# Modulation of a two-layer backbone step: from matmuls on TensorE to dot products on VectorE

## The chip, the core and the metric

The kernel runs on one core of a Trainium2 chip. Its engines run side by side, each in the order of its own queue: TensorE (PE in the profile; matmuls and transposes, results in PSUM), VectorE (DVE), ScalarE (ACT) and GpSimd (POOL). Loads are issued by SyncE (SP) and, for gathers, by GpSimd. The metric is the device time of one execution in microseconds (us).

## The reference

One step of a backbone of two layers on 384 tokens (128 context tokens, 256 latent tokens) of 1024 columns, all in float32. Each layer has a mixer and an expert stage, and each of both is modulated by a shift, a scale and a gate that depend on a conditioning vector: `c_ctx` for the context tokens, `c` for the latent ones.

```python
def adaln(cond, w, b):
    m = jax.nn.silu(cond) @ w + b                 # 1024 -> 6 * 1024
    return jnp.split(m[..., None, :], 6, axis=-1)

def modulate(x, shift, scale):
    return layer_norm(x) * (1 + scale) + shift
...
    # a layer, for either group of tokens
    h = modulate(x, shift1, scale1)
    p = h @ w_in                  # columns for three token mixers (A, B, C) and their gates
    ...                           # A: Mamba-2 scan, B: neighbourhood attention, C: grouped-query attention
    x = layer_norm(alpha * x + gate1 * mix, ...)
    ...                           # PEER: product-key routing, then 128 experts' rows per token
    x = layer_norm(alpha * x + gate2 * ffn, ...)
```

So the modulation itself is 6 vectors ("parts" 0 to 5: shift1, scale1, gate1, shift2, scale2, gate2) of 1024 numbers, for 2 layers and 2 conditioning vectors. Its cost is the weight `w_mod`: 2 x 1024 x 6144 floats, 50 MB.

## The kernel before

A layer is run in this order: the norm and modulation of its input (called the LN phase here), the mixer, `mix_out` with its norm, the routing of the PEER stage, and the PEER stage's loop over experts, which is bound by transfers. In the profiled run mixer 0 lies at about 50 to 490 us, the PEER loop of layer 0 at 740 to 1520, mixer 1 at 1560 to 1995, the PEER loop of layer 1 from 2240 on.

A mixer works through 52 blocks of 128 columns of `w_in`. For each block `load_w` (L205 ff) issues one load of 512 KB on SP's queue into a slot of the ring "w" (8 slots, which all weight loads share). `proj3` splits the block into a high and a low part: ScalarE's copy `uh` (L222), and the subtraction `ul` (L224) on VectorE (on GpSimd for the first N_FIRST = 3 blocks of a mixer). The ring "u" of splits has 3 slots. Then come 24 matmuls of 128 by 384 (L368 to L370). `split` serves `w_branch` too, in the loop of `branch` over the gate blocks. Between the blocks lies the work of the three mixers A, B and C, convolution and scan first. Each engine's order is written out at build time by a scheduler, so instructions of neighbouring steps are interleaved.

The modulation is made of 48 units (`adaln_unit`, L253), each for 256 columns: two loads of `w_mod`, 8 matmuls with the conditioning vectors as weights, `condT` (L259), a ScalarE copy `modp` (L261), two small matmuls that turn the result into columns (L265), and two ScalarE additions of the bias into `mcol` (L268). `mcol` is then read by the norms as per-channel columns.

The units are placed by `adaln(n, ...)`: 8 in the LN phase of layer 0 (shift1 and scale1 of the first mixer, two before every second channel block k); one after every second `w_in` block, in `blocks` (L373), up to N_FILL = (16, 8) in the two mixers; 4 behind the third `mix_out` of layer 0 (N_AD); 10 in the routing of layer 0, one in each `tick` from b = 6 on; and the last 2 at the same place as N_AD in layer 1.

Of the kernel before, what the change touches and what calls it, by code (L numbers as in the profile page):

```python
# [18 lines left out]
D = 1024  # L19
# [21 lines left out]
N_FILL = (16, 8)  # L41
N_AD = (4, 4)
N_END = 0
# [10 lines left out]
R_AD = 4  # L54
# [55 lines left out]

CAND = []
# [44 lines left out]
def hybrid_step(ctx: ExitStack, tc: tile.TileContext, A, O):  # L156
# [45 lines left out]
    mcol = mk(outer, [128, DEPTH, 6, KD, 2], "mcol")  # L202
# [25 lines left out]
    fill_ps, fill_n, first = [None], [0], [0]  # L228


    def cond_prep(sp, ps1):
        cond = mk(sp, [16, 128], "cond")
        dma(out=cond[0:8, :], in_=A["c_ctx"].rearrange("(k p) -> k p", p=128))
        dma(out=cond[8:16, :], in_=A["c"].rearrange("o (k p) -> (o k) p", p=128))
        V.memset(condT, 0.0)
        ps = mk(ps1, [128, 512], "pt")
        T.transpose(ps[:, :16], cond, ident[:16, :16])
        th = mk(sp, [128, 16], "cth")
        S.activation(th, ps[:, :16], AF.Tanh, scale=0.5)
        cc = mk(sp, [128, 16], "cc")  # L240
        S.activation(cc, ps[:, :16], AF.Copy, scale=0.5)
        V.scalar_tensor_tensor(condT[:, :, 0:2].rearrange("p k c -> p c k"), th.rearrange("p (c k) -> p c k", c=2), 1.0,
                               cc.rearrange("p (c k) -> p c k", c=2), op0=ALU.add, op1=ALU.mult)
        for l in range(DEPTH):
            bm = mk(sp, [48, 128], "bm", bufs=2)
            dma(out=bm, in_=A["b_mod"][l].rearrange("(k p) -> k p", p=128))
            ps = mk(ps1, [128, 512], "pt")
            T.transpose(ps[:, :48], bm, ident[:48, :48])
            V.tensor_copy(bmT[:, l], ps[:, :48])
            for part in (1, 4):  # L250
                V.tensor_scalar(bmT[:, l, part * KD:(part + 1) * KD], bmT[:, l, part * KD:(part + 1) * KD], 1.0, None, op0=ALU.add)

    def adaln_unit(l, part, hb, ps1, tags):  # L253

        w = load_k(A["w_mod"][l, part * 4 + hb])
        ps = mk(ps1, [128, 512], tags[0])
        for k in range(KD):
            q = k % 4
            T.matmul(ps[32 * q:32 * q + 32, :256], condT[:, k, :], w[k], start=(k < 4), stop=(k >= 4), tile_position=(0, 32 * q))  # L259
        mp = mk(outer, [128, 256], "modp", bufs=2)  # L260
# [3 lines left out]
        for a in range(2):  # L264
            T.matmul(pt[:, 2 * a:2 * a + 2], mp[:, a * 128:(a + 1) * 128], sel, start=True, stop=True)  # L265
        c = part * KD + 2 * hb
        for a in range(2):
            S.activation(mcol[:, l, part, 2 * hb + a, :], pt[:, 2 * a:2 * a + 2], AF.Identity, bias=bmT[:, l, c + a:c + a + 1])  # L268

    todo = []  # L270
    for l, ps in ((0, (0, 1)), (0, (2,)), (0, (3, 4)), (1, (0, 1)), (0, (5,)), (1, (2,)), (1, (3, 4)), (1, (5,))):
        todo += [(l, part, hb) for hb in range(4) for part in ps]
# [12 lines left out]

    def mod_rows(l, part, j, dst, ps1, tag, scale=1.0):

        for hb in range(2):
            ps = mk(ps1, [128, 512], tag)
            for a in range(4):  # L290
                T.matmul(ps[:, a * 128:(a + 1) * 128], mcol[:, l, part, hb * 4 + a, j:j + 1].to_broadcast([128, 128]), ident,
# [29 lines left out]
    def ln_mod_T(l, t, ish, isc, sp, xt, ps1, tag, raw, then=None):  # L321
# [3 lines left out]
        for hb in range(2):  # L325
# [5 lines left out]
            if hb == 0 or t < MOD_V:  # L331
                for q in range(4):
                    k = hb * 4 + q
                    S.activation(raw[:, k, :], ps[:, q * 128:(q + 1) * 128], AF.Identity, bias=mcol[:, l, ish, k, j:j + 1],
                                 scale=mcol[:, l, isc, k, j:j + 1])
            else:
                V.tensor_tensor(raw[:, ks, :], ps.rearrange("p (k t) -> p k t", k=4), mcol[:, l, isc, ks, j][:, :, None].to_broadcast([128, 4, 128]), op=ALU.mult)
# [1012 lines left out]
```

## Time and profile before

| | us |
|---|---|
| median of 3 runs | 3023.25 (3023.19 to 3025.1) |
| profiled execution | 3023.89 |
| its span | 3021.8 |
| TensorE busy | 2880.1 (95%) |
| VectorE busy | 2314.3 (77%) |
| ScalarE busy | 1398.6 (46%) |
| GpSimd busy | 820.5 (27%) |

The busy shares are means over stages with different bounds. The mean busy share of the DMA engines is under one half in the mixers and near full in the PEER loops. Matmuls are pipelined and their ends are modelled, so durations of neighbouring matmuls overlap in the rows; the distance from start to start is the pace.

### The profile page before, as it was taken

Reading aid. Unit: us, or ns where it says so; the run is one execution under the profiler, and the core shown is the slowest. Engines: PE = TensorE matmul, PEld = TensorE weight load, DVE = VectorE, ACT = ScalarE, POOL = GpSimd, SP = SyncE. Lnnn points to the kernel's source line nnn. Section 1 sums busy time; section 2 is a strip of 40 time slices with the busy share of each in tenths; the row PEclk is TensorE's granted clock in tenths of the full one; section 3 lists DMA queues with packets and bytes.
Section 4 is the critical chain, followed back from the end, with each engine's and each line's share of the span. In section 5 each row is a group of like instructions: output and inputs, shape, how many; then the busy total and the mean of one; then the engine's idle time right before and its main releaser. Section 6 shows DMA issues by size and latency. Waiting matters only on the chain. (4 is left out here: it accounts for less than half of the span.)

```text
span 3021.8 us, 48665 instructions
## 1 busy us (share of the span) xinstructions
PE 2880.1 (95%) x17953; PEld 2496.8 (83%) x17953; DVE 2314.3 (77%) x4888; ACT 1398.6 (46%) x2861; POOL 820.5 (27%) x566
## 2 busy tenths in 40 slices
PE   7999999999889999999969999999987999999996
PEld 5888889878779999998858888898876899999985
DVE  3745554599669999998977456446996999999988
ACT  4544542324864444444445445432168444444443
POOL 0000000101334445554530000000023444455554
PEclk9999999999999999999979999999999999999998
DMA  7445322464999999999934332124469999999994
GB/s 245 156 152 153 84 65 90 154 227 146 334 343 418 393 388 396 396 390 369 385 100 153 119 96 76 64 91 133 154 212 366 412 395 392 396 394 392 395 365 166
DMA packets 299328, 767.09 MB, mean 254 GB/s; under 512 B 42770, under 2 KB 113874, under 8 KB 299090
## 3 DMA queue, kind: packets, MB, share of 16 engines
q1 hardware_dynamic: 225362, 495.51, 46.0%
q0 software_dynamic: 73728, 268.47, 23.4%
q8 instruction: 141, 2.31, 0.3%
q14 instruction: 97, 0.79, 0.1%
HBM read 726.92 MB, written 36.96 MB: 253 GB/s over the span
## 5 line engine op out<-in xcount | busy, mean ns | idle before, releaser
L1052 POOL DMA_INDIRECT prow<-in_peer_u,ei x256 | 361.5, 1412 | 765.2 <-DVE prow L1057 521.6
L1063 POOL DMA_INDIRECT prow<-in_peer_v,ei x256 | 379.8, 1483 | 352.4 <-DVE tn L1068 310.8
L222 ACT CAST vh<-w 128x1024 fp32r<-128x1024 f32 x256 | 268.8, 1050 | 367.2 <-issue 285.6
L1162 PE MATMUL hp<-hh,uh 128*128 128x256 f32 x1488 | 433.8, 292 | 0.0
L1163 PE MATMUL hp<-hl,uh 128*128 128x256 f32 x1488 | 417.2, 280 | 0.0
L1164 PE MATMUL hp<-hh,ul 128*128 128x256 f32 x1488 | 416.8, 280 | 0.0
L1240 PE MATMUL out<-vh,al 128*128 128x512 f32 x1024 | 400.4, 393 | 3.6 <-DVE al L1225 3.6
L1239 PE MATMUL out<-vl,ah 128*128 128x512 f32 x1024 | 398.4, 391 | 3.1 <-DVE vl L224 3.1
L1238 PE MATMUL out<-vh,ah 128*128 128x512 f32 x1024 | 391.0, 398 | 1.4 <-ACT ah L1223 1.4
L224 DVE TENSOR_TENSOR vl<-w,vh 128x1024 fp32r<-128x1024 f32 x256 | 315.5, 1232 | 62.0 <-ACT vh L222 61.3
L1068 DVE SCALAR_TENSOR_TENSOR tn<-prow,pact,tn 128x1024 f32<-128x1024 f32 x254 | 325.0, 1280 | 2.7
L1150 ACT CAST uh<-w 128x1024 fp32r<-128x1024 f32 x186 | 195.4, 1051 | 251.7 <-PE hp L1163 243.0
L368 PE MATMUL pp<-hh,uh 128*128 128x384 f32 (+1 forms) x848 | 300.1, 354 | 8.9 <-ACT uh L222 4.7
L1057 DVE SCALAR_TENSOR_TENSOR prow<-prow,tn 128x1024 f32<-128x1024 f32 x256 | 302.2, 1218 | 0.3 <-DMA prow<-in_peer_u,ei 0.3
L370 PE MATMUL pp<-hh,ul 128*128 128x384 f32 (+1 forms) x848 | 296.3, 349 | 1.4 <-POOL ul L224 1.4
L1159 PE MATMUL hp<-hs,w 128*128 128x256 f32 x1120 | 266.5, 394 | 30.7 <-DMA w<-in_peer_uT 30.7
L369 PE MATMUL pp<-hl,uh 128*128 128x384 f32 (+1 forms) x848 | 295.0, 348 | 0.2 <-DVE xr L494 0.2
L1162 PEld LDWEIGHTS hp<-hh,uh 128*128 128x128 f32 x1488 | 281.3, 189 | 0.0
L1163 PEld LDWEIGHTS hp<-hl,uh 128*128 128x128 f32 x1488 | 281.2, 189 | 0.0
L1164 PEld LDWEIGHTS hp<-hh,ul 128*128 128x128 f32 x1488 | 280.4, 188 | 0.0
L1159 PEld LDWEIGHTS hp<-hs,w 128*128 128x128 f32 x1120 | 216.1, 197 | 63.0 <-DMA w<-in_peer_uT 33.5
L351 POOL TENSOR_TENSOR res<-res,lg 128x384 f32<-128x384 f32 x6 | 9.6, 1594 | 939.7 <-ACT res L313 939.7
(405 smaller groups left out, 5843.0 us busy)
## 6 DMA issues: line engine op xcount, KB each, us to landing
w<-in_peer_uT SPq DMA_DIRECT2D x256, 512.0 KB, 6.9
w<-in_peer_v SPq DMA_DIRECT2D x256, 512.0 KB, 7.2
w<-in_w_in SPq DMA_DIRECT2D x104, 512.0 KB, 3.7
w<-in_w_mod SPq DMA_DIRECT2D x96, 512.0 KB, 4.4
gd<-w SPq DMA_DIRECT2D x64, 512.0 KB, 6.1
gt<-gd SPq DMA_DIRECT2D x64, 512.0 KB, 7.4
w<-in_peer_wq SPq DMA_DIRECT2D x32, 512.0 KB, 4.4
w<-in_w_branch SPq DMA_DIRECT2D x24, 512.0 KB, 3.7
```

The costliest lines, as they stand in the source:

```text
L224: e.tensor_tensor(lo, src, hi.bitcast(F32), op=ALU.subtract)
L1052: G.indirect_dma_start(out=row, out_offset=None, in_=utab, in_offset=bass.IndirectOffsetOnAxis(ap=ei[:, j:j + 1], axis=0))
L1057: V.scalar_tensor_tensor(row, row, 1.0, tn, op0=ALU.mult, op1=ALU.mult, accum_out=hd[:, j:j + 1])
L1063: G.indirect_dma_start(out=row, out_offset=None, in_=vtab, in_offset=bass.IndirectOffsetOnAxis(ap=ei[:, j:j + 1], axis=0))
L1068: V.scalar_tensor_tensor(acc, row, act[:, j:j + 1], acc, op0=ALU.mult, op1=ALU.add)
L1159: T.matmul(o, ut[0][:, k, :], hs[:, k, :], start=(k == 0), stop=(k == KD - 1))
L1162: T.matmul(o, uh[:, k, :], hh[:, k, :], start=(k == 0), stop=False)
L1163: T.matmul(o, uh[:, k, :], hl[:, k, :], start=False, stop=False)
L1164: T.matmul(o, ul[:, k, :], hh[:, k, :], start=False, stop=(k == KD - 1))
L1238: T.matmul(o, ah[:, ts], vh[:, ns], start=f, stop=False)
L1239: T.matmul(o, ah[:, ts], vl[:, ns], start=False, stop=False)
L1240: T.matmul(o, al[:, ts], vh[:, ns], start=False, stop=e)
```

## The change

Only shift1 and scale1 of the first mixer stay on TensorE, as two units of 1024 columns (`UNITS`): 8 loads, 32 matmuls, one copy, two transposes, four additions on VectorE. They stand in the LN phase before k = 0 and k = 4. The other ten parts (`PARTS`) are made by 80 *dots* on VectorE. The host lays out these parts of `w_mod` transposed, so that a load of 512 KB holds 128 output channels on the partitions and the 1024 inputs along the row. `cond_begin` spreads both conditioning vectors over all partitions at the start of each mixer (`condr`: two loads, two tanh on ScalarE, two instructions on VectorE). A dot then takes three instructions that multiply by `condr` and sum along the row into an accumulator (`accum_out`): 512 and 512 columns for the context vector, 1024 for the other. A finished part gets two small additions. One dot stands behind every `w_in` block: N_FILL = (48, 32). The units in the mixers, behind `mix_out` and in the ticks are gone. The split ring "u" has 2 slots instead of 3. The number of bytes loaded for the modulation stays about the same (96 loads of `w_mod` before; 16 of `w_mod`, 80 of `w_modT` and 4 of `condr` now).

```diff
-N_FILL = (16, 8)
-N_AD = (4, 4)
+N_FILL = (48, 32)
+UNITS = [((0, 0, 0, 4), (0, 1, 0, 4)), ((0, 0, 4, 4), (0, 1, 4, 4))]
+PARTS = [(0, 2), (0, 3), (0, 4), (1, 0), (1, 1), (0, 5), (1, 2), (1, 3), (1, 4), (1, 5)]
...
+    dots = [(l, part, k) for l, part in PARTS for k in range(KD)]
+
+    def cond_begin(sp):
+
+        cond_rows[0] = mk(sp, [128, 2, D], "condr")
+        cond_drop[0] = mk(sp, [128, 512], "condd")
+        for c, name in enumerate(("c_ctx", "c")):
+            r = cond_rows[0][:, c]
+            dma(out=r, in_=AP(A[name], 0, [[0, 128], [1, D]]))
+            th = mk(wst, [128, RAWC], "w")
+            S.activation(th, r, AF.Tanh, scale=0.5)
+            V.scalar_tensor_tensor(r, th, 1.0, r, op0=ALU.add, op1=ALU.mult)
+
+    def adaln_dots(n):
+
+        for _ in range(min(n, len(dots))):
+            l, part, k = dots.pop(0)
+            w = mk(wst, [128, RAWC], "w")
+            dma(out=w, in_=A["w_modT"][PARTS.index((l, part)), k])
+            m = mcol[l, part]
+
+            for c, h, j in ((0, slice(0, 512), 0), (0, slice(512, D), 2), (1, slice(0, D), 1)):
+                V.scalar_tensor_tensor(w if c else cond_drop[0], w[:, h], 0.5, cond_rows[0][:, c, h], op0=ALU.mult, op1=ALU.mult, accum_out=m[:, k, j:j + 1])
+            if k == KD - 1:
+                V.tensor_tensor(m[:, :, 0], m[:, :, 0], m[:, :, 2], op=ALU.add)
...
-        wh, wl = split(wb, spool[0], "u", 3, G if first[0] >= 0 else V)
+        wh, wl = split(wb, spool[0], "u", 2, G if first[0] >= 0 else V)
...
             yield load_w(src[b0 + j])
-            if j % 2 and fill_n[0] > 0:
+            if fill_n[0] > 0:
                 fill_n[0] -= 1
-                adaln(1, fill_ps[0], ("pp", "pt"))
+                adaln_dots(1)
...
-                    if k % 2 == 0:
-                        adaln(2, ps1, ("pp", "pt"), True)
+                    if k % 4 == 0:
+                        adaln(1, ps1, ("pp", "pt"), True)
...
-        fill_ps[0], fill_n[0], first[0] = ps1, N_FILL[l], N_FIRST
+        cond_begin(pool(stack, "cnd"))
+        fill_n[0], first[0] = N_FILL[l], N_FIRST
...
             if t == 3:
-                adaln(N_AD[l] if l == 0 else len(todo), ps1, ("pp", "pp"), True)
                 next(finding)
...
-            if l == 0 and b >= N_WQ + R_AD:
-                adaln(1, pu, ("uT", "hp"), b == 15)
```

SP's queue where layer 0 ends and mixer 1 begins, before: the last loads of the PEER stage, those of `w_in` and `w_mod`, and the small loads of the mixer (`pr` to `xw`).

```order
L1133 DMA w_15608<-in_peer_v 128x1024
L210 DMA w_15858<-in_w_in 128x1024
L210 DMA w_15901<-in_w_in 128x1024
L210 DMA w_15944<-in_w_mod 128x1024
L210 DMA w_15946<-in_w_mod 128x1024
L210 DMA w_15959<-in_w_in 128x1024
L210 DMA w_16002<-in_w_in 128x1024
L210 DMA w_16045<-in_w_mod 128x1024
L210 DMA w_16047<-in_w_mod 128x1024
L210 DMA w_16065<-in_w_in 128x1024
L461 DMA pr_15823<-in_conv_w 30x128
L462 DMA pr_15823<-in_conv_b 6x128
```

The same place on SP's queue in the changed kernel.

```order
L1158 DMA w_15227<-in_peer_v 128x1024
L292 DMA condr_15435<-in_c_ctx 128x1024
L292 DMA condr_15435<-in_c 128x1024
L487 DMA pr_15455<-in_conv_w 30x128
L488 DMA pr_15455<-in_conv_b 6x128
L489 DMA pr_15455<-in_ssd_norm_g 4x128
L497 DMA dvec_15464<-in_ssd_d 64x4x1 x2
L499 DMA dtb_15467<-in_ssd_dt_bias 128x16
L501 DMA alog_15469<-in_ssd_a_log 128x16
L506 DMA xw_15471<-in_state_ssd 128x2x64 x4
L211 DMA w_15490<-in_w_in 128x1024
L302 DMA w_15533<-in_w_modT 128x1024
```

The five loads of `w_in` that stood ahead of the small loads now stand behind them, and the two `condr` loads stand ahead of all. The first of these waits until VectorE and GpSimd are through with the low part of the mixer's modulated input (`hl`).

VectorE's order in mixer 0 between convolution and scan, before: `ul` are the splits of `w_in` blocks, `xw`, `h1T` and `zT` belong to the scan.

```order
L582 SCALAR_TENSOR_TENSOR zT_889<-zh_921,zT_889 128x384
L573 TENSOR_TENSOR h1T_852<-h1T_852,pa_855 64x256 x2
L555 TENSOR_TENSOR xw_861<-xnat_824,wgt_818 128x512
L224 TENSOR_TENSOR ul_1019<-w_1015,uh_1017 128x1024
L573 TENSOR_TENSOR h1T_852<-h1T_852,pa_863 64x256 x2
L555 TENSOR_TENSOR xw_869<-xnat_824,wgt_818 128x512
L582 SCALAR_TENSOR_TENSOR zT_889<-zh_956,zT_889 128x384
L224 TENSOR_TENSOR ul_1484<-w_1480,uh_1482 128x1024
L555 TENSOR_TENSOR xw_879<-xnat_824,wgt_818 128x512
L224 TENSOR_TENSOR ul_1516<-w_1512,uh_1514 128x1024
```

The same place on VectorE in the changed kernel: `condd` and `mcol` are the outputs of a dot (L306).

```order
L581 TENSOR_TENSOR xw_810<-xnat_765,wgt_759 128x512
L306 SCALAR_TENSOR_TENSOR condd_349,mcol_10_74<-w_906,condr_348 128x512
L225 TENSOR_TENSOR ul_917<-w_913,uh_915 128x1024
L581 TENSOR_TENSOR xw_820<-xnat_765,wgt_759 128x512
L306 SCALAR_TENSOR_TENSOR w_906,mcol_10_74<-w_906,condr_348 128x1024
L308 TENSOR_TENSOR mcol_10_74<-mcol_10_74 128x8
L306 SCALAR_TENSOR_TENSOR condd_349,mcol_11_75<-w_948,condr_348 128x512
L309 TENSOR_TENSOR mcol_10_74<-mcol_10_74,bmT_85 128x8x2
L225 TENSOR_TENSOR ul_957<-w_953,uh_955 128x1024
L306 SCALAR_TENSOR_TENSOR condd_349,mcol_11_75<-w_948,condr_348 128x512
L306 SCALAR_TENSOR_TENSOR w_948,mcol_11_75<-w_948,condr_348 128x1024
```

Dots now stand between the splits, cut into their three instructions and mixed with the scan's work. Ahead of the split `ul_917` stand 39 rows of convolution, scan and dots since the split before it (`ul_875`).

## Rows read from the trace of the kernel before

**Rows 1.** Windows: start and end, length, busy us (instructions) by engine, PEclk, DMA share, GB/s
```profile
60.00:520.00 460.00, 457.92 (x2848) 390.29 (x2847) 254.10 (x546) 207.13 (x481) 1.50 (x1) 1.00 0.38 119
...
620.00:723.00 103.00, 103.00 (x626) 84.18 (x622) 101.26 (x623) 23.04 (x60) 4.86 (x5) 1.00 0.56 195
```

**Rows 2.** Windows cut at splits 0, 26, 37, 61 of mixer 0, then of mixer 1
```profile
66.08:239.33 173.25, 172.48 (x1143) 144.80 (x1141) 99.00 (x217) 85.54 (x207) 0.00 (x0) 0.99 0.49 159
239.33:324.74 85.41, 84.98 (x538) 69.98 (x535) 49.74 (x112) 40.49 (x100) 0.00 (x0) 1.00 0.49 134
324.74:484.06 159.32, 158.43 (x923) 137.09 (x922) 88.52 (x185) 69.94 (x151) 0.00 (x0) 1.00 0.24 77
1568.60:1746.26 177.66, 175.24 (x1101) 149.71 (x1100) 105.06 (x225) 84.52 (x200) 0.00 (x0) 0.97 0.43 140
1746.26:1823.90 77.64, 77.51 (x455) 65.28 (x454) 47.46 (x108) 38.95 (x91) 0.00 (x0) 1.00 0.35 90
```

**Rows 3.** Timeline of VectorE in mixer 0: start, duration, line, operation, [idle before, releaser]
```profile
212.28 1.22 DVE L224 TENSOR_TENSOR ul<-w,uh 128x1024 fp32r<-128x1024 f32 x1 [2.47 <-ACT uh L222]
216.96 1.23 DVE L224 TENSOR_TENSOR ul<-w,uh 128x1024 fp32r<-128x1024 f32 x1 [3.46 <-ACT uh L222]
223.46 1.23 DVE L224 TENSOR_TENSOR ul<-w,uh 128x1024 fp32r<-128x1024 f32 x1 [5.28 <-ACT uh L222]
```

**Rows 4.** Windows 520 to 560 and 560 to 740: L259 alone, then L265 alone (PE, PEld)
```profile
520.00:560.00 40.00, 4.94 (x64) 1.95 (x64) 0.90 0.60 207
560.00:740.00 180.00, 16.83 (x160) 5.28 (x160) 0.99 0.44 150
...
520.00:560.00 40.00, 3.08 (x16) 2.94 (x16) 0.90 0.60 207
560.00:740.00 180.00, 6.07 (x40) 5.21 (x40) 0.99 0.44 150
```

**Rows 5.** Timeline of VectorE in the PEER loop, then a group by form (busy, mean ns)
```profile
1000.74 1.22 DVE L1057 SCALAR_TENSOR_TENSOR prow<-prow,tn 128x1024 f32<-128x1024 f32 x1
1001.88 0.08 DVE L1057 DVE_READ_ACCUMULATOR prow<-prow,tn 128x1 f32 x1
1001.88 1.22 DVE L1057 SCALAR_TENSOR_TENSOR prow<-prow,tn 128x1024 f32<-128x1024 f32 x1
...
L606 DVE TENSOR_TENSOR ex<-pa,cst 128x512 f32<-128x512 f32 x24 | 16.5, 686 | 2.0 <-PE pa L600 1.7
```

**Rows 6.** ScalarE's copies of w_in blocks by form; loads, median us to landing
```profile
L222 ACT CAST uh<-w 128x1024 fp32r<-128x1024 f32 x128 | 133.8, 1048 | 168.8 <-PE pp L369 134.6 <-issue 17.5 <-PE pb L686 14.4
...
w<-in_w_in SPq DMA_DIRECT2D x104, 512.0 KB, 3.7
```

**Rows 7.** Timeline of SP's queue and of TensorE before mixer 0
```profile
30.47 2.54 SPq L210 DMA_DIRECT2D w<-in_w_in  x2
...
38.95 0.44 SPq L461 DMA_DIRECT2D pr<-in_conv_w  x1
...
44.58 1.01 PE L265 MATMUL pt<-cst,modp 128*128 128x2 f32 x4 [0.49 <-ACT modp L261]
```

**Rows 8.** Timeline of VectorE behind mix_out of layer 0 and at the routing's end
```profile
567.46 0.69 DVE L337 TENSOR_TENSOR hs<-pa,mcol 128x512 f32<-128x512 f32 x1 [7.64 <-PE pa L329]
...
729.82 0.23 DVE L969 TENSOR_SCALAR i<-ef 128x128 f32<-128x128 f32 x1 [4.06 <-PE pp L974]
```

**Rows 9.** Timeline of SP's queue and of TensorE at the start of mixer 1
```profile
1507.12 3.33 SPq L210 DMA_DIRECT2D w<-in_w_in  x2
...
1560.66 0.35 SPq L461 DMA_DIRECT2D pr<-in_conv_w  x1
...
1566.66 0.34 SPq L210 DMA_DIRECT2D w<-in_w_in  x1
...
1559.88 0.69 PE L368 MATMUL pp<-hh,uh 128*128 128x384 f32 x1 [3.83 <-ACT hh L344]
...
1571.36 0.33 PE L485 MATMUL pt<-cst,xw 128*128 128x128 f32 x1 [1.98 <-DMA xw<-in_state_ssd]
```

More of the change, by code (lines that the diff above doesn't have):

```diff
@@ L201, in hybrid_step @@
     dma(out=x[:, 1:3, :], in_=A["x_sample"][0].rearrange("(t p) d -> p t d", p=128))
-    mcol = mk(outer, [128, DEPTH, 6, KD, 2], "mcol")
+    mcol = {(l, part): mk(outer, [128, KD, 3], f"mcol{l}{part}") for l in range(DEPTH) for part in range(6)}
+    cond_rows, cond_drop = [None], [None]
     condT = mk(outer, [128, KD, 32], "condT")
@@ L238, in cond_prep @@
         th = mk(sp, [128, 16], "cth")
[L239 removed]
+        S.activation(th, cond, AF.Tanh, scale=0.5)
         cc = mk(sp, [128, 16], "cc")
[L241 removed]
+        S.activation(cc, cond, AF.Copy, scale=0.5)
         V.scalar_tensor_tensor(condT[:, :, 0:2].rearrange("p k c -> p c k"), th.rearrange("p (c k) -> p c k", c=2), 1.0,
                                cc.rearrange("p (c k) -> p c k", c=2), op0=ALU.add, op1=ALU.mult)
[L244 to L251, printed above, removed]
@@ L253, in adaln_unit @@
-    def adaln_unit(l, part, hb, ps1, tags):
-        w = load_k(A["w_mod"][l, part * 4 + hb])
+        for part in (1, 4):
+            b = bmT[:, :, part * KD:(part + 1) * KD]
+            V.tensor_scalar(b, b, 1.0, None, op0=ALU.add)
+    def adaln_unit(u, ps1, tags):
         ps = mk(ps1, [128, 512], tags[0])
         for k in range(KD):
-            q = k % 4
-            T.matmul(ps[32 * q:32 * q + 32, :256], condT[:, k, :], w[k], start=(k < 4), stop=(k >= 4), tile_position=(0, 32 * q))
-        mp = mk(outer, [128, 256], "modp", bufs=2)
+            w = mk(wst, [128, RAWC], "w")
+            dma(out=w, in_=A["w_mod"][u, k])
+            for q in range(4):
+                T.matmul(ps[32 * q:32 * q + 32, :256], condT[:, k, :], w[:, q * 256:(q + 1) * 256], start=(k == 0), stop=(k == KD - 1), tile_position=(0, 32 * q))
+        mp = mk(wst, [128, RAWC], "w")[:, :256]
@@ L264, in adaln_unit @@
         for a in range(2):
[L265 to L272, printed above, removed]
+            T.transpose(pt[:, a * 128:(a + 1) * 128], mp[:, a * 128:(a + 1) * 128], ident)
+        pv = pt[:, :256].rearrange("p (a q m) -> p q a m", a=2, q=4)
+        j = 0
+        for l, part, k0, n in UNITS[u]:
+            for c in range(2):
+                V.tensor_tensor(mcol[l, part][:, k0:k0 + n, c].rearrange("p (q a) -> p q a", a=2), pv[:, j // 2:(j + n) // 2, :, c],
+                                bmT[:, l, part * KD + k0:part * KD + k0 + n].rearrange("p (q a) -> p q a", a=2), op=ALU.add)
+            j += n
+    todo = [0, 1]
     begun = []
```

41 lines of the change are left out of this document (21 added, 20 removed).

## The prediction

> **What bounds the kernel now.** I read the span by stages first [rows 1], then the two projection stages ("mixers") cut at VectorE's weight splits [rows 2], then the timeline where the change puts or takes something. In mixer 0 TensorE is busy 457.92 of 460.00 us and VectorE 254.10: TensorE is the bound and VectorE seems to have 200 us to spare [rows 1]. From 620 to 723 us, in the stage behind the mixer, both are full: TensorE 103.00 and VectorE 101.26 of 103.00 [rows 1]. What leaves TensorE there isn't won. The cut at the splits shows what the average of mixer 0 hides: VectorE is busy 57% of its first stretch, 58% of its second, 56% of its third (99.00 of 173.25, 49.74 of 85.41, 88.52 of 159.32) [rows 2]. The cover is even over the mixer; the new work, as shown below, is not.
>
> **What a modulation unit costs on TensorE.** Splits are spaced 4.68 us apart where no unit lies between, and 6.50 us where one does [rows 3]: 1.82 us for a unit. Mixer 0 loses 16 units (29.1 us of TensorE time), mixer 1 loses 8 (14.6 us), the stage between mixer 0 and the expert loop loses 14, and the same stage of layer 1 loses 2. If all of that came back, the time would fall by well over 60 us. It can't, because the work goes to VectorE.
>
> **What a dot costs on VectorE.** A dot is three SCALAR_TENSOR_TENSOR with accumulator: 512, 512 and 1024 columns. The kernel has the 1024 form, L1057: it takes 1.22 us, and the next one starts 1.14 us later, its accumulator read included [rows 5]. For 512 columns the nearest row is a TENSOR_TENSOR of that size, 686 ns [rows 5]; with the same overlap as above it is 0.61 us from start to start, with an accumulator read (0.08 us) that isn't hidden 0.77; I take 0.70. A dot is 2 x 0.70 + 1.15 = 2.55 us, between 2.37 and 2.75. 80 dots are 204 us.
> [...]
>
> **Mixer 0, first two stretches.** Splits 0 to 37, 173.25 + 85.41 = 258.7 us [rows 2]. TensorE: 172.48 + 84.98 less 29.1 = 228 us. In VectorE's order 35 dots lie between the same two splits, since one stands behind every block: 99.00 + 49.74 + 35 x 2.55 = 238 us. So VectorE becomes the longer engine. If the two overlapped perfectly, 238 us: a gain of 20. But they are tied block by block: a projection can't run ahead of its split, the split waits in VectorE's fixed order behind dots and convolution, and the ring of split weights shrinks from 3 to 2, so that TensorE can be at most a block ahead. I added row durations along the changed order between neighbouring splits: the larger engine of each single block gives 268 us (9 us lost), the larger of each two blocks 256. The largest lump is the one that the change's section prints, with 18.7 us of VectorE work between two splits against 8.8 of TensorE's. Two slots fit the middle case: **-3 us** (-20 to +9).
>
> **Mixer 0, the rest.** Splits 37 to 61: VectorE 88.52 + 10 x 2.55 = 114 us against TensorE's 158.43, and before no unit lies here, so nothing is gained. Two slots cost something: the ScalarE copy of block b+2 (1048 ns) now waits for the end of block b, and with the 1.22 us of the subtraction that makes 2.3 us of a 4.68 us block [rows 3, 6]. It fits unless VectorE is in the middle of something: **+2** (0 to +8).
>
> **Start of mixer 0.** The two new units replace eight in a chain whose last TensorE piece (L265) starts at 44.58 us [rows 7], and should end earlier. But weight loads stood ahead of the small loads on SP's queue (two w_in at 30.47, the first small load at 38.95) [rows 7]; now the first w_in load stands behind two row loads that wait for the normed input, and behind the small loads. Gain and loss look alike: **0** (-6 to +6).
>
> **Between mixer 0 and the expert loop.** Fourteen units, 4.94 + 3.08 + 16.83 + 6.07 = 30.9 us of TensorE time [rows 4]. Most is covered by others: the four behind the third mix_out lie in a stretch where VectorE waits 7.64 us for a TensorE product (567.46) [rows 8], and after 620 VectorE is full [rows 1]. I give 4 us for the four, 4 for the two units of ticks before 620, and half of the 4.06 us in which VectorE waits for TensorE at 729.82 [rows 8]: **-10** (-17 to -4).
>
> **Start of mixer 1.** This is the loss. Before, weight loads are issued from 1507.12 us on, through the preceding tail, and the first projection starts at 1559.88, where ScalarE's copy of its input (hh) ends its wait [rows 9]. In the changed SP order the first w_in load stands behind the two row loads, which wait for that same input, and behind the small loads. Those take 6.0 us of the queue (the first at 1560.66, the next weight load at 1566.66) [rows 9]. So: 1560.7, up to 1 us for the row loads, 6.0 for the small ones, 3.7 to landing, 1.05 for the copy [rows 6]: first projection at 1572, some 12 us late. The 1.98 us that TensorE now loses to xw at 1571.36 [rows 9] is then gone: **+10** (+7 to +13).
>
> **The rest of mixer 1 and of layer 1.** Splits 0 to 26: TensorE 175.24 - 14.6 = 160.6; VectorE 105.06 + 25 x 2.55 = 169, against 177.66 before [rows 2]. With the 5% to 8% that the block-by-block sum adds to the longer engine in mixer 0: **+1** (-9 to +12). Later VectorE has 47.46 + 4 x 2.55 = 58 of 77.64 us and then no dots: TensorE bound, **+2** for the slots (0 to +8). The last two units: **-2.5** (-4 to -1).
>
> **Sum.** 0 - 3 + 2 - 10 + 10 + 1 + 2 - 2.5 = -0.5 us on the profiled run of 3023.89, and that run lies 0.6 above the median of the three shown: **3023 us**. "Same" means within 0.2%, 6 us, about what a measurement of this kernel can tell from no change.
>
> **Rivals.**
> *VectorE keeps pace (faster).* If dots fill the idle time between VectorE's splits, the longer engine alone counts: 238 us in mixer 0, 169 in mixer 1, start of mixer 1 only 7 late: -20 + 0 - 10 + 7 - 9 - 2.5 = -34, **2989 us**. For it: VectorE's even 57% and inputs of the dots that wait for nothing on TensorE. Against it: 238 exceeds 228, so there is no slack to absorb lumps.
> *The tie block by block (slower).* In-order VectorE and two slots: each block lasts as long as its slower engine. +9 in mixer 0, +9 in mixer 1, +4 and +4 for the slots, +12 for the late start, -8 and -2 outside: +28, **3051 us**. It decides from the point at which splits of the early blocks wait for VectorE more than about 0.3 us per block. For it: VectorE's lumps of several instructions per block, and the dots cut into halves among the convolution.
> [...]
>
> **How the numbers follow.** Forecast 0.50 (own range 3008 to 3037; of it 0.14 faster, 0.25 same, 0.11 slower); VectorE keeps pace 0.22, faster; block-by-block tie 0.26, of which 0.02 same; half rate 0.02. Faster 0.36, same 0.27, slower 0.37. The range takes in the block-by-block case up to 3050, and the other down to 2993.
>
> **What would show it.** After: in splits 0 to 37 of mixer 0, VectorE near 238 us busy and a window between 238 and 268; TensorE idle there on the subtraction; L306 at 1.22 us for 1024 columns and 0.6 to 0.7 for 512; the first projection of mixer 1 some 12 us behind its input; the expert loop of layer 0 starting earlier by 3 to 20 us. I am wrong if TensorE still fills mixer 0, if loads of w_in land in time for mixer 1, or if the 14 units outside the mixers give back their 31 us.

## The result: 66 us slower, and where they lie

The changed kernel takes 3088.77 us (median of 4 runs, 3085.4 to 3093.6) against 3023.22 (4 runs); the ratio is 1.022, 95% interval 1.0202 to 1.0237. The forecast was 3023, the range ended at 3050. The profiled run has a span of 3091.7 us, 69.9 more than before. Cut at the same VectorE splits as [rows 2], and at the low part of mixer 1's input (`hl`, first row at 1559.34 before, 1580.11 after), the difference lies here:

| stretch | before | after | difference | forecast |
|---|---|---|---|---|
| to split 0 of mixer 0 | 66.1 | 65.3 | -0.7 | 0 |
| mixer 0, splits 0 to 37 | 258.7 | 271.6 | +12.9 | -3 |
| mixer 0, splits 37 to 59 | 150.8 | 174.8 | +24.0 | +2 |
| from there to `hl` of mixer 1 | 1083.8 | 1068.5 | -15.4 | -10 |
| `hl` to split 0 of mixer 1 | 9.3 | 32.5 | +23.2 | +10 |
| mixer 1, splits 0 to 26 | 177.7 | 186.0 | +8.3 | +1 |
| mixer 1, splits 26 to 61 | 242.1 | 259.9 | +17.8 | +2 |
| the rest of layer 1 | 1033.4 | 1033.3 | -0.1 | -2.5 |

The windows of the changed kernel that answer to [rows 2] (columns as there; cut at splits 0, 26, 37, 59 of mixer 0, then at 0, 26, 37, 61 of mixer 1; the last line takes splits 0 to 37 of mixer 0 together):

```profile
65.34:255.08 189.74, 174.28 (x937) 149.82 (x937) 155.97 (x378) 79.39 (x178) 0.00 (x0) 0.90 0.47 148
255.08:336.89 81.81, 76.73 (x442) 63.23 (x441) 70.36 (x172) 37.16 (x87) 0.00 (x0) 1.00 0.59 165
336.89:511.65 174.76, 162.07 (x921) 135.76 (x920) 109.55 (x248) 67.96 (x147) 0.00 (x0) 0.99 0.32 98
1612.61:1798.56 185.95, 168.74 (x935) 146.10 (x936) 155.90 (x378) 79.51 (x178) 0.00 (x0) 0.93 0.48 150
1798.56:1891.74 93.18, 86.17 (x483) 69.60 (x482) 61.59 (x151) 40.58 (x98) 0.00 (x0) 0.96 0.42 114
1891.74:2058.47 166.73, 159.63 (x920) 137.32 (x918) 85.33 (x173) 66.88 (x139) 0.00 (x0) 1.00 0.23 76
...
65.34:336.89 271.55, 251.01 (x1377) 213.04 (x1377) 226.33 (x547) 116.54 (x264) 0.00 (x0) 0.93 0.51 153
```

The kernel before between splits 37 and 59 of mixer 0:

```profile
324.74:475.52 150.78, 149.89 (x874) 128.66 (x873) 83.93 (x179) 67.10 (x148) 0.00 (x0) 1.00 0.24 77
```

Three things are to be seen. VectorE's work in splits 0 to 37 of mixer 0 is near the forecast: 226.33 us with its 35 dots (238 worked out). The time is not: 271.55 us is more than either engine's busy time, and the longer engine is TensorE, busy 251.01 us where 228 were worked out. And in the first stretch of either mixer the granted clock of TensorE is 0.90 and 0.93, where it was 0.99 and 0.97. TensorE is busy 174.28 us with 937 matmuls there; before, 172.48 us held 1143. The largest loss lies where the forecast saw next to none, in the late stretches: +24.0 us behind split 37 of mixer 0 and +17.8 behind split 26 of mixer 1.

The dots' durations (group by form; min/median/max ns), which answer to [rows 5]:

```profile
L306 DVE SCALAR_TENSOR_TENSOR condd<-w,condr x160: 661/685/2740, 49.0 to 1816.8; 128x512 f32<-128x512 f32 x160
L306 DVE SCALAR_TENSOR_TENSOR w<-w,condr x80: 1204/1218/1228, 54.4 to 1818.1; 128x1024 f32<-128x1024 f32 x80
```

### The profile page after: what moved, and what is told of

The parts are those of the page before. It is cut to its first block, busy times and chain, and to the rows that moved or that the text cites. A ratio compares the mean times of both kernels' runs of the same rounds, so it can differ in the third digit from the quotient of the medians.

```text
span 3091.7 us, 47328 instructions
## 1 busy us (share of the span) xinstructions
PE 2842.9 (92%) x17122; PEld 2475.4 (80%) x17122; DVE 2509.2 (81%) x5396; ACT 1371.1 (44%) x2723; POOL 822.4 (27%) x566
## 4 chain that ended last, share of the span: by engine, by line
PE 62%; DVE 20%; DMA 6%; ACT 6%; issue 4%; POOL 1%; SPq 0%; POOLq 0%; ACTq 0%; DVEq 0%
PE hp L1188 6%; PE hp L1187 6%; PE out L1263 6%; PE out L1262 6%; PE hp L1189 6%; PE out L1261 6%; PE pp L393 3%; PE pp L395 3%; PE pp L394 3%; DMA w<-in_peer_uT 2%; ACT ol L1025 2%; PE hp L1184 2%; DVE vl L225 2%; DVE ul L225 2%; PE hp L1242 1%
## 5 line engine op out<-in xcount | busy, mean ns | idle before, releaser
L395 PE MATMUL pp<-hh,ul 128*128 128x384 f32 (+1 forms) x848 | 300.9, 355 | 17.9 <-DVE ul L225 15.0
L393 PE MATMUL pp<-hh,uh 128*128 128x384 f32 (+1 forms) x848 | 301.4, 355 | 14.3 <-ACT uh L223 11.4
L1184 PE MATMUL hp<-hs,w 128*128 128x256 f32 x1120 | 274.5, 403 | 33.2 <-DMA w<-in_peer_uT 27.0
```

Source lines behind the costliest of these rows:

```text
L393: T.matmul(o, wh[:, k, :], hh[:, k, :], start=(k == 0), stop=False)
L395: T.matmul(o, wl[:, k, :], hh[:, k, :], start=False, stop=(k == KD - 1))
L1184: T.matmul(o, ut[0][:, k, :], hs[:, k, :], start=(k == 0), stop=(k == KD - 1))
```

## The low clock of the early stretch

In mixer 0 between splits 0 and 17 the changed kernel's granted clock is 0.87. Two windows of 10 us in it and behind it show what that means for the pace (same columns):

```profile
65.34:211.13 145.79, 131.64 (x688) 109.50 (x688) 118.39 (x302) 58.59 (x137) 0.00 (x0) 0.87 0.38 121
...
180.00:190.00 10.00, 10.00 (x37) 8.02 (x37) 5.13 (x18) 0.90 (x2) 0.00 (x0) 0.50 0.10 41
210.00:220.00 10.00, 10.00 (x63) 9.63 (x62) 9.21 (x18) 6.02 (x10) 0.00 (x0) 1.00 0.58 179
```

Both of the short windows are full; the one at a clock of 0.50 holds 37 matmuls, the one at 1.00 63. Matmuls of one form, `pp` with 384 columns, start 0.32 us apart in the first and 0.17 us in the second. So in this kernel a busy TensorE is not a fast one. What it did before the clock fell: it had waited, for VectorE above all (11.8 us of the 14.2 that it is idle between splits 0 and 17); the last long wait ahead of the window at 0.50 took 2.06 us and ended at 177.09. The waits of TensorE between splits 0 and 17 (the row ahead of the window at 0.50; then what it waited for, us in total, times, longest):

```profile
177.09 0.40 PE L647 MATMUL pa<-w,xnat 128*64 128x128 f32 x2 [2.06 <-DVE w L645]
...
PE pp L395 <- DVE ul L225: 4.3, 4, 1.7
PE pa L593 <- DVE xw L581: 3.0, 2, 1.9
PE pa L647 <- DVE w L645: 2.9, 3, 2.1
PE pa L587 <- DVE xw L581: 1.6, 1, 1.6
```

The longest wait is 2.06 us, and 10 of the 14 waits are for VectorE, none for a load. The low clock stands among these waits (0.87 between splits 0 and 17, 0.50 from 180 to 190 us); that they bring it about is not shown by these rows.

## The experiments

The runs were made on several chips, each beside the kernel before, whose median there lay between 3022.6 and 3029.1 us; a ratio is to that. A difference of two runs' times is therefore good to some 6 us.

**The shorter ring alone.** The kernel before, with

```diff
-        wh, wl = split(wb, spool[0], "u", 3, G if first[0] >= 0 else V)
+        wh, wl = split(wb, spool[0], "u", 2, G if first[0] >= 0 else V)
...
-                wh, wl = split(load_w(A["w_branch"][l, i, hb], 4), spool[0], "u", 3)
+                wh, wl = split(load_w(A["w_branch"][l, i, hb], 4), spool[0], "u", 2)
```

> The kernel before with one edit: the ring of split weights has 2 slots instead of 3; all modulation units stay on TensorE. If the shorter ring is what cost the late stretches of the mixers (splits 37 to 59 of mixer 0 took 163.8 us instead of 150.8, splits 26 to 61 of mixer 1 took 259.9 instead of 242.1), this kernel loses about as much there: 25 to 35 us, 3048 to 3058 us in all. If the dots on VectorE are the cause there too, and the ring is only a detail, it stays within 8 us of the kernel before: 3023 to 3031.

3060.29 us, ratio 1.011 (1.0089 to 1.0131): 34 us above the kernel before on that chip. Splits 0 to 59 of mixer 0 take 433.2 us instead of 409.4, of mixer 1 421.0 instead of 411.2. The ScalarE copies of w_in blocks between splits 26 and 59 of mixer 0 show how (idle us before them, by what ended it; times). In the kernel before:

```profile
  PE pp L369: 16.9, 7
```

With two slots:

```profile
  PE pp L369: 40.6, 11
```

The copy (of a w_in or a w_branch block) waits for TensorE to be through with the block whose slot it takes. In the gate blocks a split of w_branch holds one slot over two projections, so two slots leave one for the projections, and copy and subtraction (1.05 and 1.22 us) can't lie beside the block that they follow. VectorE is light there (busy 80.67 of 160.83 us between splits 37 and 59 of mixer 0 with two slots), and it costs all the same: the ring theory holds, and its upper end (3058) was even passed. In the late stretches the ring takes 10.1 us (splits 37 to 59 of mixer 0) and 11.5 us (26 to 61 of mixer 1) of the 24.0 and 17.8; another 13.7 us lie in splits 0 to 37 of mixer 0 (272.3 against 258.7), where the expectation did not look for it. (The 163.8 us that it gives for splits 37 to 59 of the changed kernel are cut one split late; between these splits it is 174.8 us.)

**Three slots in the changed kernel.** Besides the slots: conditioning rows and the unused output in float16, the rows loaded through two more slots of the weight ring, two attention buffers (`pT`, `bt`) with 2 copies instead of 3.

```diff
-        wh, wl = split(wb, spool[0], "u", 2, G if first[0] >= 0 else V)
+        wh, wl = split(wb, spool[0], "u", 3, G if first[0] >= 0 else V)
...
-        cond_rows[0] = mk(sp, [128, 2, D], "condr")
+        cond_rows[0] = mk(sp, [128, 2, D], "condr", dt=F16)
...
```

> The changed kernel with 3 slots in the ring of split weights. To make room, the conditioning rows are kept in float16 (so the modulation is rounded), the unused output of a dot is float16, and two small attention buffers have 2 copies instead of 3. Ring theory: 25 to 35 us of the 66 come back, 3054 to 3064 us. VectorE theory: VectorE's order is the bound, and a third slot gives back 0 to 10 us: 3079 to 3089.

3058.97 us, ratio to before 1.011 (1.0089 to 1.0132): 30 us of the 66 come back. They come back in another place than expected (splits 0 to 59): mixer 0 gains 3.4 us (446.3 to 442.9), mixer 1 27 (437.2 to 410.3), the start of mixer 1 12 (32.5 to 20.6). Within mixer 0 splits 0 to 37 gain 11.4 us (271.6 to 260.1) and splits 37 to 59 lose 8.0 (174.8 to 182.7). The smaller attention buffers have a price there: TensorE waits 10.9 us in the two mixers for the loads of `bt`, and not at all with 3 copies in the changed kernel.

**No dots.** The changed kernel without dots, their loads and the conditioning rows, with 2 slots, then with 3:

```diff
-N_FILL = (48, 32)
+N_FILL = (0, 0)
...
-        cond_begin(pool(stack, "cnd"))
```

> The changed kernel without the dots: neither their loads, nor the conditioning rows, nor their work on VectorE are there (the modulation apart from the first shift and scale is a constant, so the output is not the reference's). Two slots in the ring. VectorE theory: without dots TensorE bounds the mixers again and all units are off it, so the mixers fall by 29 and 15 us below before, and the stages outside keep their 18 and 4 us: about 2960 us. Ring theory: the same, less the 25 to 35 us of the ring: 2985 to 2995.

> The changed kernel without the dots, their loads and the conditioning rows (the modulation apart from the first shift and scale is a constant), and with 3 slots in the ring of split weights. The kernel without dots and with 2 slots took 2997 us. Ring theory: 25 to 35 us less, as it cost the kernel before: 2962 to 2972. If the ring costs only where another engine is late, it costs nothing beside a light VectorE: 2990 to 2997.

2997.26 us (ratio 0.9904, 0.9884 to 0.9925) and 2970.08 (0.9811, 0.9782 to 0.984). So the ring costs 27 us even with no dot, and the dots, with their loads and rows, cost 92 us with two slots. Ring theory (2985 to 2995, then 2962 to 2972) is missed by 2 us in the first run and met in the second. Splits 0 to 59 of either mixer, added up step by step:

| | mixer 0 | mixer 1 |
|---|---|---|
| kernel before | 409.4 | 411.2 |
| no dots, three slots | 394.4 | 397.0 |
| no dots, two slots | 405.5 | 408.6 |
| changed kernel | 446.3 | 437.2 |

Taking the units away gives 15 and 14 us, the slot takes 11 and 12, and the dots take 41 and 29: within the mixers the dots cost most. With three slots and no dots splits 0 to 17 of mixer 0 read:

```profile
48.62:160.39 111.77, 110.22 (x666) 94.84 (x664) 86.11 (x203) 59.14 (x140) 0.00 (x0) 1.00 0.28 93
```

With two slots, as in the changed kernel:

```profile
55.21:175.45 120.24, 117.10 (x705) 100.29 (x704) 84.50 (x204) 59.50 (x140) 0.00 (x0) 0.99 0.25 77
```

Beside the changed kernel's 145.79 us the second, which differs from it in the dots and their rows alone, gives the parts of the early loss: about as many matmuls (705 and 688) keep TensorE busy 117 us at a clock of 0.99 and 132 us at 0.87, and idle time goes from 3.1 to 14.2 us. The low pace is the larger part of the difference (14.5 of 25.6 us), the waits themselves the smaller (11.0).

**The loads' order at the start.** In the changed kernel the tanh of the conditioning rows takes two slots of the weight ring, and the loads of w_in come behind them in the ring. Here it takes the small tile instead:

```diff
-            th = mk(wst, [128, RAWC], "w")
-            S.activation(th, r, AF.Tanh, scale=0.5)
-            V.scalar_tensor_tensor(r, th, 1.0, r, op0=ALU.add, op1=ALU.mult)
+            for h in (slice(0, 512), slice(512, D)):
+                S.activation(cond_drop[0], r[:, h], AF.Tanh, scale=0.5)
+                V.scalar_tensor_tensor(r[:, h], cond_drop[0], 1.0, r[:, h], op0=ALU.add, op1=ALU.mult)
```

> The changed kernel, but the tanh of the conditioning rows goes through the small tile for unused outputs in halves, not through two slots of the weight ring. In the order of SyncE's queue the first five loads of w_in then stand ahead of the conditioning rows again, in both layers. If the late start of mixer 1 (first VectorE split 32.5 us behind the split of its input, 9.3 before) is due to this order, 15 to 23 us come back: 3066 to 3074. If mixer 1 is bound by VectorE anyway, an earlier start of TensorE is lost again: 3083 to 3089.

3078.37 us (ratio 1.0178, 1.0154 to 1.0202), 10 less. SP's queue at the start of mixer 1 in the changed kernel:

```profile
1581.46 0.33 SPq L292 DMA_DIRECT2D condr<-in_c_ctx  x1
...
1588.63 0.45 SPq L211 DMA_DIRECT2D w<-in_w_in  x1
1591.59 0.34 SPq L302 DMA_DIRECT2D w<-in_w_modT  x1
1591.97 0.43 SPq L211 DMA_DIRECT2D w<-in_w_in  x1
```

The same in this one:

```profile
1511.95 0.33 SPq L211 DMA_DIRECT2D w<-in_w_in  x1
...
1571.74 0.33 SPq L292 DMA_DIRECT2D condr<-in_c_ctx  x1
```

Loads begin 60 us before the conditioning rows instead of 7 behind them, and from `hl` to split 0 it takes 13.5 us instead of 32.5. Of these 19 us, mixer 1 loses 11 again (splits 0 to 59: 448.6 against 437.2). Both theories were half right: the order is the cause of the late start of mixer 1, and an early start is partly absorbed by what bounds the mixer. In mixer 0 the order alone is not the cause: the loads of w_in stand ahead of the rows there too (27.71 us against 34.63), and split 0 still starts at 65.12.

**Both repairs.** Three slots, and the rows fetched behind the fifth w_in block:

```diff
+            if e == 4:
+                cond_begin()
+            n = 1 if e > 4 else 0
...
-                adaln_dots(1)
+            adaln_dots(n)
```

> The changed kernel with 3 slots (with the same room made as in the run with three slots) and with the conditioning rows fetched behind the fifth w_in block, where the dots begin too. If the costs of ring, load order and dots add up, 3059 less 10 to 19 us: 3040 to 3049. If VectorE is the bound, an earlier start is absorbed: 3054 to 3059.

3052.18 us (ratio 1.0085, 1.0057 to 1.0113): 7 below the run with three slots, between the two ranges, so this run decides for neither theory. Of the 66 us, 29 are left, and 82 against the kernel without dots and with three slots. That kernel has 3 copies of the attention buffers; here TensorE waits 10.1 us for loads of `bt` in the mixers, there 0, so up to some 10 of the 82 us belong to the buffers and not to the dots. Split 0 of mixer 0 now starts at 49.66 us. The next runs change this kernel.

**The place of the dots.** As many dots, but few behind the first 18 blocks (and in mixer 1 the rows fetched behind the eighteenth):

```diff
+            if e < 18:
+                n = 1 if len(dots) > 32 and e > 4 and e % 3 == 2 else 0
+            else:
+                n = 2 if len(dots) > 32 and e >= 28 and e % 3 == 0 else 1
```

> As the run with 3 slots and rows last, but the same number of dots stands elsewhere: in mixer 0 only 5 dots behind the first 18 blocks, then one per block, and in the last 24 blocks four behind three; in mixer 1 no dot behind the first 18 blocks, then one per block. If the place of the dots is what costs (VectorE behind the first blocks is full of convolution and scan, and idle in the last blocks), most of the loss goes: 2980 to 3005 us. If their amount on VectorE costs wherever they stand, it stays within 10 us of the run with 3 slots and rows last: 3035 to 3050.

3019.05 us, ratio 0.9993 (0.9977 to 1.0009): 33 us less for the same dots, and the same as the kernel before. It lies between the two ranges: the place costs, but it accounts for less than half of the 82 us. Splits 0 to 17, then 37 to 59 of mixer 0:

```profile
49.19:156.85 107.66, 106.05 (x640) 93.29 (x639) 97.75 (x234) 57.50 (x130) 0.00 (x0) 1.00 0.42 141
293.62:477.04 183.42, 166.86 (x925) 140.51 (x924) 138.63 (x332) 70.39 (x154) 0.00 (x0) 0.94 0.40 128
```

The early stretch is as fast as without dots. But the late one is 28 us longer than without (155.4), though VectorE is busy only 138.63 of its 183.42 us. The forecast's price for dots beside TensorE-bound blocks, nothing, is wrong there too.

**Half the VectorE work.** Only the 1024-column instruction of each dot:

```diff
-            for c, h, j in ((0, slice(0, 512), 0), (0, slice(512, D), 2), (1, slice(0, D), 1)):
+            for c, h, j in ((1, slice(0, D), 1),):
```

> As the run with 3 slots and rows last, but each dot makes only its 1024-column instruction for the latent tokens (the values for the context tokens are a constant): the loads stay, the VectorE work of the dots halves. VectorE theory: the cost of the dots falls by a half or more, 2995 to 3015 us. If their loads or their slots in the ring of weights cost, it stays: 3035 to 3050.

3018.39 us (ratio 0.9983, 0.9971 to 0.9995): 34 of the 82 us for half of the work, less than the half that VectorE theory asked for (3015 was its end), but far from no change. Splits 0 to 61 fall by 19.0 us in mixer 0 (453.7 to 434.7) and 26.2 in mixer 1 (443.5 to 417.3).

**The dots without their loads.** The dots read the mixer's input `hh` instead of a loaded weight; the slots of the weight ring are taken as before:

```diff
-            dma(out=w, in_=A["w_modT"][PARTS.index((l, part)), k])
+            src = cond_src[0].rearrange("p k t -> p (k t)").bitcast(F32)
...
```

> As the run with 3 slots and rows last (3052 us), but the dots read a tile that is there already instead of a weight load: same instructions on VectorE at the same places, same slots of the weight ring, no loads of w_modT (the modulation is wrong). If VectorE's time is what the dots cost, it stays: 3044 to 3056 us. If their loads cost (VectorE waited 18.6 us for them in the changed kernel, and loads of w_in stand behind them), 15 to 30 us come back: 3022 to 3037.

3023.71 us (ratio 1.0008, 0.9997 to 1.0018): 28 less than with loads. Splits 0 to 17 and about 37 to 59 of mixer 0 with loads (three slots, rows last):

```profile
49.66:191.49 141.83, 131.33 (x721) 112.48 (x720) 117.26 (x293) 63.99 (x146) 0.00 (x0) 0.90 0.37 120
302.98:494.80 191.82, 175.47 (x957) 145.85 (x956) 128.28 (x306) 73.53 (x165) 0.00 (x0) 0.94 0.34 109
```

The same without loads:

```profile
49.33:190.31 140.98, 129.63 (x728) 111.58 (x727) 121.09 (x303) 64.78 (x147) 0.00 (x0) 0.92 0.20 67
302.23:475.56 173.33, 164.65 (x944) 139.37 (x943) 121.60 (x284) 71.91 (x160) 0.00 (x0) 0.97 0.22 68
```

In mixer 0 the runs divide the stretches between the theories: the early one doesn't care for the loads (141.83 and 140.98), the late one gains 18 us without them (and 18 more, to 155.4, without the dots themselves). In mixer 1 the early stretch gains too, from 145.86 to 130.87 us. By which way the loads cost, the ring, the queue or the small attention loads behind them, isn't settled.

**Work added to TensorE where it idles.** The changed kernel, and behind each dot the 8 matmuls of a former unit, on data that is there, used by nobody:

```diff
+                ps = mk(fil[1], [128, 512], "pp")
+                for k in range(KD):
+                    q = k % 4
+                    T.matmul(ps[32 * q:32 * q + 32, :256], condT[:, k, :], fil[0][:, k, :256].bitcast(F32), start=(k < 4), stop=(k >= 4), tile_position=(0, 32 * q))
```

> The changed kernel with idle work added on TensorE: behind each of the 80 dots the 8 column-tiled matmuls of a former unit, without load, copy or use (about 1.1 us each, 88 us in all, some 28 of them between splits 0 and 17 of mixer 0). In the changed kernel that stretch took 145.8 us with a granted clock of 0.87. If the low clock is what TensorE's gaps cost there, the fillers raise the clock and pay for themselves: stretch at most 146 us, clock above 0.95, and the kernel less than 45 us longer in all. If the clock is only a sign of TensorE's waiting and costs nothing, the stretch is 155 us or more.

3127.81 us in all (ratio to before 1.0331, 1.0314 to 1.0348), 39 more than the changed kernel (34 by the two ratios); the later blocks carry fillers too. But splits 0 to 17 of mixer 0:

```profile
65.19:201.14 135.95, 134.42 (x941) 103.53 (x939) 117.39 (x298) 58.04 (x137) 0.00 (x0) 0.99 0.41 130
```

253 matmul rows more (a filler's 8 matmuls show as 16 rows), the same VectorE work, a clock of 0.99 instead of 0.87, and the stretch is 10 us shorter (135.95 against 145.79; in mixer 1 136.9 against 142.2). All bounds of the first theory were met, which speaks for a clock that is more than a sign. Two things weaken this: the order in which VectorE does that work was written out anew and is another one, and by split 26, with fillers behind each dot, the gain is spent (193.86 against 189.74).

The same fillers in the first 18 blocks only, with three slots and rows last:

```diff
+            if n and e < 18:
+                ps = mk(fil[1], [128, 512], "pp")
...
```

> As the run with 3 slots and rows last (3052 us; stretch from split 0 to 17 of mixer 0 141.8 us at a granted clock of 0.90, of mixer 1 145.9 at 0.87), with the idle filler matmuls behind the first 18 blocks of each mixer only. If the low clock is the larger part of the early stretches' loss, the stretches fall by 5 to 15 us in spite of 14 us more work, and the kernel by 10 to 25: 3027 to 3042 us. If VectorE's order alone sets the stretches, they stay, and the kernel is within 6 us of 3052.

3045.26 us (ratio 1.0085, 1.0067 to 1.0103), 7 less than without, about what the spread of those runs can tell, and between the two ranges. In mixer 1 splits 0 to 17 fall from 145.86 to 132.22 us (clock 0.87 to 1.00), in mixer 0 they stay (141.83 and 142.40) though the clock goes from 0.90 to 0.99:

```profile
47.68:190.08 142.40, 141.64 (x944) 112.22 (x943) 119.24 (x296) 63.04 (x144) 0.00 (x0) 0.99 0.38 130
1578.81:1711.03 132.22, 131.35 (x893) 104.24 (x893) 115.89 (x289) 59.98 (x141) 0.00 (x0) 1.00 0.40 137
```

So in three of four stretches the fillers shorten splits 0 to 17, by 5 to 14 us; in the fourth they cost what they brought. In mixer 1 of this run the gain lasts: splits 0 to 61 take 429.7 us instead of 443.5. That a part of the early loss is the clock's is made likely by this, but not shown apart from the order of the instructions, which moves with the fillers; how large the part is stays open.

**One part of the change alone.** The kernel before, with the two big units, and the conditioning and bias laid out by the host; everything else as before:

```diff
-                    if k % 2 == 0:
-                        adaln(2, ps1, ("pp", "pt"), True)
+                    if k % 4 == 0:
+                        adaln(1, ps1, ("pp", "pt"), True)
...
```

> The kernel before with one part of the change alone: shift and scale of the first mixer are made by the two units of 1024 columns, with the conditioning vectors and the bias laid out by the host. The other 40 units stay on TensorE and at their places, and the ring of split weights keeps 3 slots; there are no dots. In the runs with 3 slots and early w_in loads VectorE's first split of mixer 0 starts at 49 us instead of 66. If that comes from the two units, this kernel gains 10 to 17 us: 3006 to 3014 us, and it beats both kernels. If it comes from the loads that those runs don't have at the start, it stays within 6 us of the kernel before.

3018.57 us, ratio 0.9985 (0.9976 to 0.9995): 0.15% below the kernel before. It beats both kernels, as the first theory said, but by less than that theory's 10 us. Split 0 of mixer 0 starts at 50.97 instead of 66.08; of these 15 us, splits 0 to 59 lose 5 (414.5 against 409.4), and the profiled span is 5.4 shorter (3016.4). The part of the change that pays was priced at 0. In the changed kernel it doesn't show (its split 0 starts at 65.34), nor with the loads of w_in ahead of the rows (65.12); it does without rows and dots (55.21) and with the rows behind the fifth block (49.66). So the rows at the start hide it, and which of their parts does isn't settled.

**Mixtures.** 16 dots per mixer (5 behind the first 18 blocks, then one per block), and 24 units on TensorE, 10 of them in the mixers: first among the gate blocks, then early. A unit's copy `modp` takes a slot of the weight ring here, not a buffer of its own as in the kernel before.

```diff
+            n = 1 if (e < 18 and e > 4 and e % 3 == 2) or 18 <= e < 29 else 0
+            if e >= 30 and e % 2 and u_fill[0] > 0:
+                u_fill[0] -= 1
+                small(1, fill_ps[0], ("pp", "pt"))
...
```

> A mixture: 3 slots, rows last, big units at the start, and only 16 dots in each mixer, where they cost least in the run with dots in light stretches (5 behind the first 18 blocks, then one per block); the other 24 units stay on TensorE, 14 of them in the stage between mixer 0 and the expert loop. If the cost of dots grows with their number in a stretch, the 32 dots cost some 10 us and the 24 units some 29, on top of 2970: 3004 to 3012, faster than both kernels. If the cost per dot is the same everywhere (49 us for 80), 3018 to 3024.

```diff
-            if e >= 30 and e % 2 and u_fill[0] > 0:
+            if 7 <= e < 22 and e % 2 and u_fill[0] > 0:
```

> As the run with few dots, but the 10 units inside the mixers stand between the 8th and 18th w_in block instead of between the last blocks, where each stretch of 11 splits was 26 us longer with them than without any modulation. If the place of the units was the fault there, and 16 dots per mixer are free behind the first 29 blocks, about 35 to 45 us less than 3058: 3010 to 3023, perhaps below the kernel before. If the mixture as such costs (two rings' loads alternate), it stays above 3040.

3058.46 us (ratio 1.0103, 1.0086 to 1.012) and 3093.88 (1.0247, 1.0232 to 1.0263): both guesses were wrong; the second run is above 3040 as its other theory said, but 35 us slower than the first run. In the first, splits 0 to 26 of mixer 0 take 159.4 us, 161.4 without any modulation: the dots are free there. But the next stretch takes 103.8 us against 77.6: TensorE is busy 92.9 us with 538 matmuls (77.5 with 455), and it waits 7.8 us for loads of `bt`. In the second, splits 0 to 17 take 156.1 us:

```profile
48.28:204.41 156.13, 142.47 (x786) 120.06 (x785) 105.81 (x248) 67.76 (x159) 0.00 (x0) 0.85 0.31 109
```

Clock 0.85 again, with VectorE busy only two thirds. The engines wait for each other there (us in total, times, longest):

```profile
PE pa L694 <- DVE w L692: 6.3, 6, 2.8
DVE xc L702 <- PE pa L700: 23.0, 8, 7.1
```

What starts this isn't known. That `modp` goes through the weight ring is an untested rival to the place of the units.

## Why the prediction was wrong, point by point

**The late stretches: +2 and +2, each between 0 and +8; measured +24.0 and +17.8.** This is the largest miss, and two steps failed in it. The first is the price of the two slots. The step "it fits unless VectorE is in the middle of something" took 2.3 us of copy and subtraction against a block of 4.68 us, as if each projection had two slots for itself. In the gate blocks it has one. Alone, the ring costs 34 us on the kernel before and 27 on the kernel without dots, of the 34 us 10.1 and 11.5 in the two late stretches. The second is the step that dots beside a TensorE-bound stretch cost nothing. In the kernel with three slots and the rows last, splits 37 to 59 take 191.8 us, without the loads of the dots 173.3, without dots 155.4, though neither engine is full there. The prediction has no term for the loads, and priced the dots' work in that place at nothing because VectorE's 114 us lie below TensorE's 158.

**Splits 0 to 37 of mixer 0: -3, between -20 and +9; measured +12.9.** VectorE's busy time came out a little under the sum (226 us against 238), and the dots' durations were right: 685 ns for 512 columns and 1218 for 1024. The step that failed is TensorE's 228 us: "the larger engine of each single block" let TensorE work at its pace whenever it works. It was busy 251.0 us at a clock of 0.93 (0.87 up to split 17) and idle 20.5, so VectorE did not become the longer engine, and the stretch passed the upper bound of 268 us by 3.6. The slot has a part in this too: with three slots the same stretch takes 260.1 us, +1.5, inside the range. The lumps were where the prediction put them: the split behind the 18.7 us lump came 17.9 us later than before (107.22 against 89.33).

**The start of mixer 1: +10, between +7 and +13; measured +23.2.** The mechanism was right, and the queue's part as well: w_in is issued 7.2 us behind the conditioning rows (7 worked out). The step that failed counted the first load alone, with its median landing. The first projection started 15.8 us behind `hl`, not 12:

```profile
1580.11 1.29 DVE L370 TENSOR_TENSOR hl<-hraw,hh 128x512 fp32r<-128x512 f32 x2 [0.68 <-ACT hh L369]
...
1594.82 1.04 ACT L223 CAST uh<-w 128x1024 fp32r<-128x1024 f32 x1 [2.16 <-DMA w<-in_w_in]
...
1595.92 0.69 PE L393 MATMUL pp<-hh,uh 128*128 128x384 f32 x1 [1.80 <-ACT uh L223]
1598.35 0.69 PE L395 MATMUL pp<-hh,ul 128*128 128x384 f32 x1 [1.42 <-POOL ul L225]
...
1605.45 2.40 POOL L225 TENSOR_TENSOR ul<-w,uh 128x1024 fp32r<-128x1024 f32 x1 [4.37 <-ACT uh L223]
```

Then the next blocks came one by one, each with its load, its copy and a GpSimd subtraction of 2.4 us; before, the first of these three subtractions stood ahead of `hl` (1552.86) and the other two back to back (1560.85 and 1563.18). `hl` to split 0 is the interval that should have been priced.

**The stage behind mixer 0: -10, between -17 and -4; measured -15.4.** Right in sign and inside its range. The waits of [rows 8] are nearly gone: VectorE waits 2.12 us at L362 (7.64 before) and 0.30 at L995 (4.06 before):

```profile
587.05 0.69 DVE L362 TENSOR_TENSOR hs<-pa,mcol 128x512 f32<-128x512 f32 x1 [2.12 <-PE pa L354]
...
743.73 0.23 DVE L995 TENSOR_SCALAR i<-ef 128x128 f32<-128x128 f32 x1 [0.30 <-PE pp L1000]
```

I had given back only half of the second, and nothing of what lies between. The interval also holds the tail of mixer 0, so it isn't the stage alone.

**Start of mixer 0: 0; measured -0.7.** Right as a sum of gain and loss, but by luck in size: the run of the start alone gains 15 us, outside the bound of 6, and something at the start takes the 15 back. The order of w_in and row loads, which the prediction named, is not it alone (65.12 with the old order).

**Splits 0 to 26 of mixer 1: +1, between -9 and +12; measured +8.3.** Inside its range.

**The rivals.** The half rate, with 0.02 of the chances, is shown by no run: a dot's 1024 columns took 1218 ns, where L1057 [rows 5] and the plain subtraction of that size [rows 3] took 1.22 us. The block-by-block tie (3051) was nearest: its +9 for the early stretches stands beside the measured +12.9 and +8.3, its +4 for each late stretch beside +24.0 and +17.8. What made the range too narrow is that the terms for the late stretches, for splits 0 to 37 and for the start of mixer 1 were outside their own ends, all on the same side.

## What to carry to other kernels

Before work is moved to an engine with idle time, look at what the move takes along: a buffer slot given up to make room (34 us here), scratch tiles that go through a ring which also prefetches (10 us), and the loads (28 us). An engine with idle time is not one whose time is free: the dots, with their loads and rows, took 41 and 29 us of the two mixers. Price a shorter ring at the place where the fewest slots are left for the step in question, not at the plain loop. And here TensorE, which had to wait for the receiver, lost twice, 11.0 us of an early stretch by the waits and 14.5 by a slower pace, at a clock of 0.87 instead of 0.99: read the granted clock of the stretch beside its busy time.

## What the hardware showed that I had not expected

Waits of at most 2.1 us each, some 14 us in a stretch of 146, came with a granted clock of 0.87; beside the kernel without dots and with two slots the lower pace accounts for 14.5 us of the longer stretch, the waits for 11.0. In the run with 253 useless matmul rows more the clock was 0.99 and the stretch 10 us shorter.

The 512-column instruction of a dot took up to 2740 ns (median 685). The two long ones of mixer 0 stand beside GpSimd's first splits (so do the two of mixer 1):

```profile
49.05 2.51 DVE L306 SCALAR_TENSOR_TENSOR condd<-w,condr 128x512 f32<-128x512 f32 x1 [1.78 <-DMA w<-in_w_modT]
51.60 2.73 DVE L306 SCALAR_TENSOR_TENSOR condd<-w,condr 128x512 f32<-128x512 f32 x1
...
48.65 2.35 POOL L225 TENSOR_TENSOR ul<-w,uh 128x1024 fp32r<-128x1024 f32 x1 [48.20 <-ACT uh L223]
51.34 2.44 POOL L225 TENSOR_TENSOR ul<-w,uh 128x1024 fp32r<-128x1024 f32 x1 [0.34 <-ACT uh L223]
```

Either instruction ends 0.55 or 0.56 us behind the split beside it (51.56 against 51.00, 54.33 against 53.78; in mixer 1 1598.85 against 1598.29 and 1601.63 against 1601.08). The next 512-column instruction, with no split beside it, starts at 55.53 and takes 0.69 us. That the split holds the dot up, and by what, isn't shown.
